# Three moves in a two-layer hybrid kernel: decay rates behind the substitution, chunk outputs in the transposes' banks, attention's value products in groups of four

## The chip, the cores and the metric

The kernel runs on one core of one Trainium2 chip. The metric is device time in microseconds (us). The kernel before took 876.38, 877.22 and 877.27 us in three runs, so its median is 877.22 us. One further execution was profiled; all durations below come from that one.

## The reference

Two layers run over 512 tokens of width 1024. Each layer normalises its input, projects it by one wide matrix, sends the pieces through three mixers of 512 channels (8 heads of 64), gates and normalises what they give, projects it back and adds it to the stream:

```python
for l in range(DEPTH):                       # 2 layers
    proj = rms_norm(h, ln_g[l]) @ w_in[l]
    u_a, z_a, u_b, z_b, q_lat, kv_lat, k_rope, z_c = jnp.split(proj, pts, axis=-1)
    y_a = rwkv7_mix(u_a, ...)                # S = S*w - (S kk) b + v k, one step a token
    y_b = rms_norm(rglru_mix(u_b, ...))      # h_t = a_t h_(t-1) + bx_t, a channel each
    y_c = rms_norm(mla_mix(q_lat, kv_lat, k_rope, ...))   # causal softmax attention
    h = h + concat([y_a*silu(z_a), y_b*silu(z_b), y_c*silu(z_c)]) @ w_out[l]
return rms_norm(h, final_g)
```

In `rglru_mix` the decay is `a = exp(-8 * gate_r * softplus(-lam))`. The vector `softplus(-lam)` depends on parameters alone, so one computation serves both layers.

## The kernel before, in words

**Arithmetic.** Each wide product is made of three matmuls (`mm3`, L231 to L233) over a high and a low half of each operand. The halves of a weight tile come from a copy on ScalarE (L140) and a subtraction on GpSimd or VectorE (L227). Some 5700 matmuls pass through TensorE (PE in the profile).

**Banks.** Matmul results go to eight banks. A rotating pool `ps` has two and serves mostly the transposes, `ck()` hands out two fixed banks in turn, and `acc` has four for the wide sums. Work on a bank waits until all that read its last contents are done.

**Order.** A compile-time scheduler lays out one instruction list for each engine from the order in which the program is written, strings of step letters and the dependences; at run time each engine takes its list strictly in order. An instruction that waits therefore holds up all behind it on its engine.

**Decay rates.** `decay_rates()` (L257 to L278) computes `softplus(-lam)` for 8 columns once, in layer 0: an exponential on ScalarE, and 25 small operations on VectorE (DVE), among them a series of seven multiply and add pairs (L272, L273). It stands behind the first list of steps of the layer. The last mask products of that list (`products`: matmuls L610, masks L613 on VectorE, transposes L628) come next on VectorE.

**Chunk stage.** The delta-rule mixer is worked in 8 chunks of 64 tokens. `substitute()` inverts 32 small triangular blocks on VectorE (L738, L740, then the transposes L743 and L745 and the copies L749). It is followed by corner products (L758, L770) and by `chunk()`: `uo` (L848) multiplies the state S, L851 adds it to the values, `so` (L858) with L862 and L863 makes the next state. After each second chunk come the outputs `yo` (L876 and L882, two banks), which VectorE copies (L884) and ScalarE squares (L885). Between these, projections and the second mixer are laid: its gate products (L688), `lru_b` (exponentials, square roots, L703 to L721, the scan L713, the squares L719 summed on GpSimd by L720), the token sums over those squares (L378), and the products for the attention's latents, which take the four `acc` banks at once.

**Attention.** For four head pairs, softmax rows are made from the scores (L1057), transposed per key block (L1076), copied by ScalarE into one of four slots (L140), and multiplied with the values (L1082) into one bank, each head into 64 of its 128 rows. Parts of the output projection are filled in between.

Of the kernel before, what the change touches and what calls it, by code (L numbers as in the profile page):

```python
# [47 lines left out]
def body(ctx, tc, x, wc, wl, wo, w2a2, gagx, wuq, wukv, vec, ln_g, fin_g, cst, out, depth=DEPTH):  # L48
# [49 lines left out]
    def ck(shape=(128, 512)):  # L98
        ckn[0] += 1
        n = 1  # L100
        for s in shape[1:]:
            n *= s
        o = cks[:, ckn[0] % 2, 0:n]
        if len(shape) == 3:
            return o.rearrange("p (a b) -> p a b", a=shape[1])
        if len(shape) == 4:
            return o.rearrange("p (a b c) -> p a b c", a=shape[1], b=shape[2])
        return o
# [11 lines left out]
    cur = [None]  # L120
    SETS = {"S": "sigmoid_and_others", "E": "natural_log_exp_and_others", "Q": "sqrt_and_others"}
    NOSYNC = mybir.DependencyInfo(mybir.DependencyClass.NoSync, mybir.DependencyReason.DATA)

    def chained(ins):
        ins = getattr(ins, "ins", ins)
# [134 lines left out]
    def decay_rates():  # L260

        lam = vecs[:, :, VO["lam"]:VO["lam"] + 4]
        l0, l1, l2, l3 = [sm([128, DEPTH, 4]) for _ in range(4)]
        V.scalar_tensor_tensor(out=l0, in0=lam, scalar=-1.0, in1=lam, op0=ALU.mult, op1=ALU.min)
        act(l1, l0, AF.Exp)
        V.tensor_scalar(out=l2, in0=l1, scalar1=2.0, scalar2=None, op0=ALU.add)
        V.reciprocal(out=l3, in_=l2)
        V.tensor_tensor(out=l1, in0=l1, in1=l3, op=ALU.mult)
        V.tensor_tensor(out=l2, in0=l1, in1=l1, op=ALU.mult)
        V.tensor_scalar(out=l3, in0=l2, scalar1=1.0 / 17.0, scalar2=1.0 / 15.0, op0=ALU.mult, op1=ALU.add)  # L270
        for n in (13, 11, 9, 7, 5, 3, 1):
            V.tensor_tensor(out=l3, in0=l3, in1=l2, op=ALU.mult)  # L272
            V.tensor_scalar(out=l3, in0=l3, scalar1=1.0 / n, scalar2=None, op0=ALU.add)  # L273
        V.tensor_tensor(out=l3, in0=l3, in1=l1, op=ALU.mult)
        V.tensor_scalar(out=l0, in0=lam, scalar1=-1.0, scalar2=0.0, op0=ALU.mult, op1=ALU.max)
        V.scalar_tensor_tensor(out=l0, in0=l3, scalar=2.0, in1=l0, op0=ALU.mult, op1=ALU.add)
        V.tensor_scalar(out=sp8, in0=l0, scalar1=8.0, scalar2=None, op0=ALU.mult)
        V.tensor_scalar(out=nsp8, in0=l0, scalar1=-8.0, scalar2=None, op0=ALU.mult)  # L278
# [41 lines left out]
    def one_layer(l):  # L320
# [328 lines left out]
        run(ORD1)  # L649


        if l == 0:
            decay_rates()
        wmod[0] = WA
        gza = []

# [68 lines left out]
        def substitute():  # L725

            X, X0 = cks.rearrange("p a (t s) -> p (a t) s", s=32), c4([128, 32, 32])
            V.transpose(out=X0.rearrange("p t s -> p (t s)"), in_=inv["D"].rearrange("p t s -> p (t s)"))
            V.tensor_copy(out=X, in_=X0)
            TT = inv["T"] = c8([128, 32, 64])  # L730
            for q in (1, 3):
                G.memset(TT[32 * q:32 * q + 32, :, 0:32], 0.0)
            tm = tl("xt", [128, 240])
            for k in range(1, 31):
                n = 31 - k
                tv = tm[:, 0:n * k].rearrange("p (t s) -> p t s", t=n)

                V.tensor_tensor(out=tv, in0=X0[:, k + 1:32, k:k + 1].to_broadcast([128, n, k]),  # L738
                                in1=X[:, k:k + 1, 0:k].to_broadcast([128, n, k]), op=ALU.mult)
                V.tensor_tensor(out=X[:, k + 1:32, 0:k], in0=X[:, k + 1:32, 0:k], in1=tv, op=ALU.add)  # L740
            V.memset(X.rearrange("p t s -> p (t s)")[:, 0:1024:33], 1.0)
            X1 = inv["X1"] = c4([128, 32, 32])
            V.transpose(out=X1.rearrange("p s y -> p (s y)"), in_=X.rearrange("p t s -> p s t"))  # L743
            TD = inv["TD"] = c4([128, 32, 32])
            V.transpose(out=TD.rearrange("p s t -> p t s"), in_=X.rearrange("p t s -> p (t s)"))  # L745
            for q in range(4):
                rows = slice(32 * q, 32 * q + 32)
                blk = q % 2
                V.tensor_copy(out=TT[rows, :, blk * 32:(blk + 1) * 32], in_=TD[rows])  # L749

        def corner_left(hf):
            go = ck([128, 16, 32])
# [87 lines left out]
        def chunk(ch):  # L840
            cp, par = ch // 2, ch % 2
            ur = slice(64 * (1 - par), 64 * (1 - par) + 64)
            if ch:
                uo = [ck([128, 4, 64]) for _ in range(2)]
                for p in range(4):
                    for e in range(2):
                        hr = slice(64 * e, 64 * e + 64)
                        PE.matmul(uo[e][ur, p, :], AR[p][hr, 0, ch * 64:(ch + 1) * 64], S[ch][hr, p, :], start=True, stop=True)  # L848
                for e in range(2):
                    u = UV[ur, :, ch, 64 * e:64 * e + 64]  # L850
                    V.tensor_tensor(out=u, in0=uo[e][ur, :, :], in1=u, op=ALU.add)  # L851
            if ch < 7:
                so = ck([128, 4, 64])
                for p in range(4):
                    for e in range(2):
                        hr = slice(64 * e, 64 * e + 64)
                        hc = slice(e * 64, (e + 1) * 64)
                        PE.matmul(so[hr, p, :], BT[p][:, ch, hc], UV[:, p, ch, hc], start=True, stop=True)  # L858
                sn = S[ch + 1] = tl("S", [128, 4, 64], bufs=3)
                pc = PC[:, :, ch:ch + 1].to_broadcast([128, 4, 64])  # L860
                if ch:
                    V.tensor_tensor(out=sn, in0=so, in1=S[ch], op=ALU.add)  # L862
                    V.tensor_tensor(out=sn, in0=sn, in1=pc, op=ALU.mult)  # L863
                else:
                    V.tensor_tensor(out=sn, in0=so, in1=pc, op=ALU.mult)
            if par == 0:
                return
            yt = c2([128, 4, 2, 64])
            sq = c2([128, 4, 2, 64])
            yo = [ck([128, 4, 64]) for _ in range(2)]  # L870

            for p in range(4):
                for e, q in ((0, 0), (1, 1), (0, 1), (1, 0)):
                    hr, uq, c = slice(64 * e, 64 * e + 64), slice(64 * q, 64 * q + 64), 2 * cp + q
                    if c:
                        PE.matmul(yo[e][uq, p, :], AR[p][hr, 1, c * 64:(c + 1) * 64], S[c][hr, p, :], start=p == 0, stop=False)  # L876
            for e in range(2):
                hc = slice(e * 64, (e + 1) * 64)
                for p in range(4):
                    for q in range(2):  # L880
                        uq, c = slice(64 * q, 64 * q + 64), 2 * cp + q
                        PE.matmul(yo[e][uq, p, :], AM[q][:, p * 8 + e * 4 + cp, 64:128], UV[:, p, c, hc], start=c == 0 and p == 0, stop=p == 3)  # L882
            for e in range(2):
                V.tensor_copy(out=yt[:, :, e, :], in_=yo[e])  # L884
                A.activation(out=sq[:, :, e, :], in_=yo[e], func=AF.Square)  # L885
            V.tensor_reduce(out=vr[:, cp, :, :], in_=sq, axis=AX.X, op=ALU.add)
            yts.append(yt)
# [180 lines left out]
        def heads(p, fill):  # L1068
            ot = ck()
            for kt in range(4):  # L1070
                n = (4 - kt) * 128
                pts = []
                for e in range(2):
                    o = ps()
                    for qt in range(kt, 4):
                        PE.transpose(o[:, (qt - kt) * 128:(qt - kt + 1) * 128], Pm[p][e, qt][:, kt * 128:(kt + 1) * 128], ident)  # L1076
                    pt = PT[:, 2 * (kt % 2) + e, :]
                    copy(pt[:, 0:n], o[:, 0:n])
                    pts.append(pt)
                fill[kt]()  # L1080
                for e in range(2):
                    PE.matmul(ot[e * 64:(e + 1) * 64, kt * 128:T], Vt[:, kt, 2 * p + e, :], pts[e][:, 0:n], start=(kt == 0), stop=(kt == 3))  # L1082
            if p == 0:
                A.activation(out=stc, in_=ot, func=AF.Square)
            else:
                sq = g2()
                A.activation(out=sq, in_=ot, func=AF.Square)
                G.tensor_tensor(out=stc, in0=stc, in1=sq, op=ALU.add)
            y = g2()
            V.scalar_tensor_tensor(out=y, in0=ot, scalar=vc("mla_g", p), in1=gzc[p], op0=ALU.mult, op1=ALU.mult)  # L1090
            yc.append(y)
# [129 lines left out]
```

## Time and profile before

| what | number |
|---|---|
| median of the runs | 877.22 us |
| the profiled execution | 874.97 us |
| its span | 873.2 us |
| TensorE busy | 804.3 us, 92% of the span |
| VectorE busy | 578.5 us, 66% |
| ScalarE busy | 502.5 us, 58% |
| GpSimd busy | 333.3 us, 38% |

The profile gives for each engine when an instruction started, how long it took, how long the engine stood idle ahead of it, and what ended that idle time. Times count from the start of the span. What decides here is the idle time of TensorE, and the few stretches in which its granted clock falls, since it is busy nearly everywhere else. Layer 0 and layer 1 run the same instruction lists but for small differences, so that a stretch of the one can be laid beside its twin in the other.

### The profile page before, as it was taken

To read this page: it belongs to the slowest core of one execution; us is meant where nothing else is said; L and a number is where in the kernel's file an instruction comes from. 1 tells how busy PE (TensorE), PEld (TensorE's weight loads), DVE (VectorE), ACT (ScalarE), POOL (GpSimd) and SP (SyncE) were. 2 spreads that over 40 slices of the span, in tenths; PEclk is the share of its full clock that TensorE was granted. 3 is DMA by queue.
4 is the path that set the end of the run, shared out by engine and by line. 5 is a ranking of instruction groups with operands and counts; after the bars stand their busy time and mean duration, and the time that the engine had idled before them with its cause. 6 is when DMAs were issued, how large, how long until landed. Compare 5 with 4: busy or idle time off the path is not lost.

```text
span 873.2 us, 15237 instructions
## 1 busy us (share of the span) xinstructions
PE 804.3 (92%) x5696; PEld 619.0 (71%) x5696; DVE 578.5 (66%) x1176; ACT 502.5 (58%) x988; POOL 333.3 (38%) x303
## 2 busy tenths in 40 slices
PE   3999997999888988999979999999999898899995
PEld 3878886886668867555768788888765696665574
DVE  5678787824887385874474776786268767677636
ACT  5667874456653535564465677845665445365634
POOL 2355554532443342010534655664133533310223
PEclk9999998999999999999999999999999999999998
DMA  6322232410112365222653222332101224731344
GB/s 221 112 73 72 70 103 86 137 62 26 42 33 91 117 209 182 72 70 94 213 190 97 73 88 91 97 112 92 38 26 41 76 95 148 235 103 49 110 166 158
DMA packets 49755, 91.08 MB, mean 104 GB/s; under 512 B 5520, under 2 KB 8336, under 8 KB 49680
## 3 DMA queue, kind: packets, MB, share of 16 engines
q1 hardware_dynamic: 49104, 89.05, 31.7%
q8 instruction: 45, 0.74, 0.4%
q10 hardware_dynamic: 576, 1.05, 0.3%
q14 instruction: 30, 0.25, 0.1%
HBM read 73.30 MB, written 16.78 MB: 103 GB/s over the span
## 4 chain that ended last, share of the span: by engine, by line
PE 64%; DVE 18%; ACT 8%; DMA 5%; issue 3%; POOL 2%; SPq 0%; ACTq 0%; DVEq 0%; POOLq 0%
PE acc L231 14%; PE acc L232 14%; PE acc L233 13%; PE acc L1057 4%; PE ck L1082 3%; PE ps L1076 3%; ACT g L137 3%; PE ps L688 2%; DMA dr<-hp 2%; DVE g L721 1%; DVE g L682 1%; DVE g L713 1%; ACT UV L140 1%; ACT wH L140 1%; PE ps L628 1%
## 5 line engine op out<-in xcount | busy, mean ns | idle before, releaser
L227 POOL TENSOR_TENSOR wL<-wr,wH 128x512 fp32r<-128x512 f32 (+1 forms) x130 | 176.1, 1359 | 308.2 <-ACT wH L140 284.4
L140 ACT ACTIVATE wH<-wr 128x512 fp32r<-128x512 f32 (+1 forms) x192 | 118.8, 621 | 144.9 <-PE acc L232 72.5
L231 PE MATMUL acc<-xH,wH 128*128 128x512 f32 (+1 forms) x496 | 193.4, 391 | 0.0
L232 PE MATMUL acc<-xL,wH 128*128 128x512 f32 (+1 forms) x496 | 189.7, 383 | 0.1
L233 PE MATMUL acc<-xH,wL 128*128 128x512 f32 (+1 forms) x496 | 189.5, 382 | 0.0
L231 PEld LDWEIGHTS acc<-xH,wH 128*128 128x128 f32 x496 | 94.8, 191 | 19.7 <-issue 1.6
L233 PEld LDWEIGHTS acc<-xH,wL 128*128 128x128 f32 x496 | 94.6, 191 | 18.9 <-issue 1.6
L232 PEld LDWEIGHTS acc<-xL,wH 128*128 128x128 f32 x496 | 94.8, 191 | 16.6 <-DVE xL L305 0.6
L227 DVE TENSOR_TENSOR wL<-wr,wH 128x512 fp32r<-128x512 f32 (+1 forms) x62 | 48.3, 779 | 64.7 <-ACT wH L140 64.5
L231 PE MATMUL acc<-wH,c 128*128 128x512 f32 x192 | 81.6, 425 | 5.3 <-DVE hp L427 5.3
L232 PE MATMUL acc<-wL,c 128*128 128x512 f32 x192 | 76.4, 398 | 0.5 <-DVE wL L227 0.5
L233 PE MATMUL acc<-wH,c 128*128 128x512 f32 x192 | 75.8, 397 | 0.0
L140 ACT ACTIVATE UV<-ps 64x512 f32<-64x512 f32 (+4 forms) x112 | 52.1, 494 | 40.4 <-PE ps L1076 31.2
L231 PEld LDWEIGHTS acc<-wH,c 128*128 128x128 f32 x192 | 36.1, 188 | 17.0 <-DVE hp L427 4.1
L140 ACT ACTIVATE c<-g 128x512 fp32r<-128x512 f32 (+1 forms) x40 | 24.8, 630 | 33.2 <-DVE g L980 27.6
L137 ACT ACTIVATE c<-acc,sm 128x128 f32<-128x128 f32 (+3 forms) x64 | 33.6, 527 | 17.8 <-DVE sm L1059 17.6
L232 PEld LDWEIGHTS acc<-wL,c 128*128 128x128 f32 x192 | 36.2, 189 | 8.6 <-issue 1.4
L1057 PE MATMUL acc<-am,am 128*128 128x128 f32 (+3 forms) x128 | 41.3, 444 | 1.1 <-ACT c L137 1.1
L233 PEld LDWEIGHTS acc<-wH,c 128*128 128x128 f32 x192 | 36.0, 188 | 8.5 <-issue 1.0
L137 ACT ACTIVATE g<-g 128x512 f32<-128x512 f32 (+1 forms) x58 | 36.2, 627 | 6.1 <-DVE g L706 4.2
L135 ACT ACT_TABLE_LOAD x29 | 37.2, 1283 | 1.2 <-PEq L1209 0.7
L368 POOL TENSOR_TENSOR g<-g,g 128x512 f32<-128x512 f32 x24 | 33.2, 1382 | 11.9 <-ACT g L137 11.9
(222 smaller groups left out, 1596.9 us busy)
## 6 DMA issues: line engine op xcount, KB each, us to landing
wr<-in_wc_dram SPq DMA_DIRECT2D x116, 256.0 KB, 2.6
wr<-in_wo_dram SPq DMA_DIRECT2D x48, 256.0 KB, 3.4
hp<-dr SPq DMA_DIRECT2D x40, 256.0 KB, 3.5
dr<-hp SPq DMA_DIRECT2D x32, 256.0 KB, 3.1
dr<-g SPq DMA_DIRECT2D x16, 256.0 KB, 2.3
g<-dr SPq DMA_DIRECT2D x16, 256.0 KB, 3.7
wr<-in_wl_dram SPq DMA_DIRECT2D x16, 208.0 KB, 2.5
c<-in_x_dram SPq DMA_DIRECT2D x8, 256.0 KB, 6.3
```

The lines of the kernel that those rows point to most:

```text
L135: chained(A.preload_act_table_set(SETS[st]))
L137: chained(A.activation(out=out, in_=in_, func=func, **kw))
L140: i = A.activation(out=out, in_=in_, func=AF.Copy, **kw)
L227: (V if wn[0] % wmod[0] == 0 else G).tensor_tensor(out=L, in0=raw, in1=f(H), op=ALU.subtract)
L231: PE.matmul(o, a[0], b[0], start=start, stop=False)
L232: PE.matmul(o, a[0], b[1], start=False, stop=False)
L233: PE.matmul(o, a[1], b[0], start=False, stop=stop)
L368: G.tensor_tensor(out=z, in0=z, in1=s, op=ALU.mult)
L688: PE.matmul(o[hr, :], gw[hr, w, j, :], xc[hr, :], start=True, stop=True)
L1057: PE.matmul(o[:, 0:n], qT[:, hd, qt * 128:n], K2[:, p, e, 0:n], start=True, stop=True)
L1076: PE.transpose(o[:, (qt - kt) * 128:(qt - kt + 1) * 128], Pm[p][e, qt][:, kt * 128:(kt + 1) * 128], ident)
L1082: PE.matmul(ot[e * 64:(e + 1) * 64, kt * 128:T], Vt[:, kt, 2 * p + e, :], pts[e][:, 0:n], start=(kt == 0), stop=(kt == 3))
```

## The change

There are three edits.

1. `decay_rates()` is called at the end of `substitute()` of layer 0 in place of behind the first list of steps, and its series is written with fused operations, 18 on VectorE where there were 25.
2. The outputs `yo` of a chunk pair take two banks of the rotating pool `ps` in place of `ck()`.
3. The value products of the attention are issued for two key blocks and both heads together, after the fill of the odd key block. The first of the four gets a dependence on the last of the four copies into the slots.

```diff
@@ decay_rates
-        V.tensor_scalar(out=l3, in0=l2, scalar1=1.0 / 17.0, scalar2=1.0 / 15.0, op0=ALU.mult, op1=ALU.add)
-        for n in (13, 11, 9, 7, 5, 3, 1):
-            V.tensor_tensor(out=l3, in0=l3, in1=l2, op=ALU.mult)
-            V.tensor_scalar(out=l3, in0=l3, scalar1=1.0 / n, scalar2=None, op0=ALU.add)
-        V.tensor_tensor(out=l3, in0=l3, in1=l1, op=ALU.mult)
+        V.tensor_scalar(out=l3, in0=l2, scalar1=1.0 / 17.0, scalar2=None, op0=ALU.mult)
+        for n in (15, 13, 11, 9, 7, 5, 3):
+            V.scalar_tensor_tensor(out=l3, in0=l3, scalar=1.0 / n, in1=l2, op0=ALU.add, op1=ALU.mult)
+        V.scalar_tensor_tensor(out=l3, in0=l3, scalar=1.0, in1=l1, op0=ALU.add, op1=ALU.mult)
@@ after run(ORD1)
-        if l == 0:
-            decay_rates()
@@ substitute, at its end
+            if l == 0:
+                decay_rates()
@@ chunk
-            yo = [ck([128, 4, 64]) for _ in range(2)]
+            yo = [ps([128, 4, 64]) for _ in range(2)]
@@ heads
-                pts = []
                 for e in range(2):
                     o = ps()
                     for qt in range(kt, 4):
                         PE.transpose(...)
-                    pt = PT[:, 2 * (kt % 2) + e, :]
-                    copy(pt[:, 0:n], o[:, 0:n])
-                    pts.append(pt)
+                    last_pt = copy(PT[:, 2 * (kt % 2) + e, 0:n], o[:, 0:n])
                 fill[kt]()
-                for e in range(2):
-                    PE.matmul(ot[e * 64:(e + 1) * 64, kt * 128:T], Vt[:, kt, 2 * p + e, :], pts[e][:, 0:n], start=(kt == 0), stop=(kt == 3))
+                if kt % 2 == 0:
+                    continue
+                for k2 in (kt - 1, kt):
+                    for e in range(2):
+                        i = PE.matmul(ot[e * 64:(e + 1) * 64, k2 * 128:T], Vt[:, k2, 2 * p + e, :], PT[:, 2 * (k2 % 2) + e, 0:(4 - k2) * 128],
+                                      start=(k2 == 0), stop=(k2 == 3))
+                        if k2 < kt and e == 0:
+                            tc.add_manual_dep(i.ins, last_pt.name, SYNC, reason="one group")
```

The scheduler lays the lists out anew. In the changed kernel's file most lines are one number higher at first (L231 is L232, L613 stays) and two lower from `gate_a` on (L688 is L686, L705 is L703).

**VectorE, layer 0, ahead of the last mask products.** Before (`am` is the masked product, `sm` the 8 columns of the decay rates):

```order
L594 TENSOR_TENSOR g_169_789<-ps_1200,g_187_873 128x512
L272 TENSOR_TENSOR sm_1210<-sm_1210,sm_1209 128x8
L210 TENSOR_TENSOR c_319_1505<-g_220_1027,c_318_1504 128x512
L273 TENSOR_SCALAR sm_1210<-sm_1210 128x8
...
L274 TENSOR_TENSOR sm_1210<-sm_1210,sm_1208 128x8
L276 SCALAR_TENSOR_TENSOR sm_1207<-sm_1210,sm_1207 128x8
L277 TENSOR_SCALAR sp_102<-sm_1207 128x8
L278 TENSOR_SCALAR nsp_103<-sm_1207 128x8
L613 TENSOR_TENSOR am_317<-ps_1336,C 128x512
```

With the change, the same place:

```order
L592 SCALAR_TENSOR_TENSOR g_220_1027<-g_220_1027,vecs,g_229_1069 128x512
L594 TENSOR_TENSOR g_169_789<-ps_1200,g_187_873 128x512
L211 TENSOR_TENSOR c_315_1475<-g_220_1027,c_314_1474 128x512
L613 TENSOR_TENSOR am_317<-ps_1306,C 128x512
L613 TENSOR_TENSOR am_317<-ck,C 128x512
```

The small operations have left the place ahead of the first mask product; they now stand between the last steps of the substitution and behind its transposes.

**TensorE, layer 0, at the token sums.** `acc_2798` to `acc_2801` before, and `acc_2801` to `acc_2804` with the change, are the four banks of the latents. Before, the sums (L378) stand between products of all four, behind the last chunk:

```order
L231 MATMUL acc_2801<-wH_2842,xH_104 128x416
L232 MATMUL acc_2801<-wL_2843,xH_104 128x416
L233 MATMUL acc_2801<-wH_2842,xL_105 128x416
L231 MATMUL acc_2798<-wH_2860,xH_104 128x416
L232 MATMUL acc_2798<-wL_2861,xH_104 128x416
L378 MATMUL ck<-ones_96,sqn_2232 128x2 x4
```

With the change (`ps_3130` are the first transposes of the chunk outputs):

```order
L234 MATMUL acc_2803<-wH_2863,xL_105 128x416
L978 MATMUL ps_3130<-C,c_406_2267 128x128
L978 MATMUL ps_3130<-C,c_412_2342 128x128
L978 MATMUL ps_3130<-C,c_432_2484 128x128
L978 MATMUL ps_3130<-C,c_437_2556 128x128
L378 MATMUL ck<-ones_96,sqn_2227 128x2 x4
L232 MATMUL acc_2804<-wH_2809,xH_104 128x416
L233 MATMUL acc_2804<-wL_2810,xH_104 128x416
```

All products of the fourth bank, and half of those of the other three, now stand behind the token sums. The gate products of `lru_b(2, 3)`, on whose results the sums depend, moved from between the second and third chunk pairs to behind the last chunk; between them and the sums stand 12 matmuls of 512 columns and 36 of 416, beside the transposes shown. On VectorE and ScalarE the work of `lru_b(2, 3)` moved behind the last chunk in the same way.

**TensorE, layer 0, first head pair of the attention.** Before, each key block's two products (L1082) stand together:

```order
L1057 MATMUL acc_3754<-am_3119,am_3121 128x512
L231 MATMUL acc_3763<-wH_3606,c_550_3134 128x512
L232 MATMUL acc_3763<-wL_3607,c_550_3134 128x512
L233 MATMUL acc_3763<-wH_3606,c_550_3134 128x512
L1082 MATMUL ck<-UV_3120 64x384 x2
L1076 MATMUL ps_3770<-C,c_654_3557 128x128
```

With the change the products are L1083:

```order
L1057 MATMUL acc_3755<-am_3122,am_3124 128x512
L1083 MATMUL ck<-UV_3123 64x512
L232 MATMUL acc_3764<-wH_3609,c_558_3137 128x512
L233 MATMUL acc_3764<-wL_3610,c_558_3137 128x512
L234 MATMUL acc_3764<-wH_3609,c_558_3137 128x512
L1083 MATMUL ck<-UV_3123 64x512
L1083 MATMUL ck<-UV_3123 64x384 x2
L1075 MATMUL ps_3777<-C,c_664_3562 128x128
```

The first product of a group stands alone and the other three follow together after other matmuls, in the first three head pairs; the 256 and 128 column products of the later key blocks stand together in all four.

More of the change, by code (lines that the diff above doesn't have):

```diff
@@ L122, in body @@
     NOSYNC = mybir.DependencyInfo(mybir.DependencyClass.NoSync, mybir.DependencyReason.DATA)
+    SYNC = mybir.DependencyInfo(mybir.DependencyClass.Sync, mybir.DependencyReason.DATA)
     def chained(ins):
```

## The prediction

> **What bounds the kernel now.** I read the page first, then the waits of TensorE (PE), then stretches of the timeline, with layer 1 beside layer 0.
>
> ```profile
> span 873.2 us, 15237 instructions
> PE 804.3 (92%) x5696; PEld 619.0 (71%) x5696; DVE 578.5 (66%) x1176; ACT 502.5 (58%) x988; POOL 333.3 (38%) x303
> PE ck L848 <- ACT c L885: 12.8, 4, 4.3
> PE ps L628 <- DVE am L613: 6.1, 3, 5.0
> ```
>
> TensorE is busy 92% of the span, so an edit pays by the idle time of TensorE that it removes, or by matmul time. A row of waits gives total, times and longest. Two of them bear on the change: 12.8 us ahead of L848, where a chunk wants a bank from which ScalarE has not yet squared the outputs, and 6.1 us ahead of L628, behind masks that VectorE (DVE) is late with. Stages that no edit names keep their work, with the order a little shifted; I take nothing for them.
>
> **Decay rates.** Columns are start, duration, engine, line, operation, count, and in brackets the idle time before.
>
> ```profile
> 131.10 1.25 DVE L273 TENSOR_SCALAR sm<-sm 128x8 f32<-128x8 f32 x1
> 136.20 0.17 DVE L272 TENSOR_TENSOR sm<-sm,sm 128x8 f32<-128x8 f32 x1
> 138.38 0.68 DVE L613 TENSOR_TENSOR am<-ps,C 128x512 f32<-128x512 f32 x1
> 139.12 1.11 PE L628 MATMUL ps<-C,c 128*128 128x128 f32 x4 [4.98 <-DVE am L613]
> 132.09 0.37 PE L610 MATMUL ps<-c,c 64*128 64x128 f32 x1
> 563.05 0.37 PE L610 MATMUL ps<-c,c 64*128 64x128 f32 x1
> 169.15 2.02 PE L785 MATMUL ps<-UV,am 64*64 64x64 f32 x62
> 592.31 0.86 PE L785 MATMUL ps<-UV,am 64*64 64x64 f32 x22
> 130.00:140.00 10.00, 5.02 (x38) 4.04 (x36) 9.49 (x21) 4.33 (x8) 6.07 (x5) 0.92 0.46 158
> 140.00:150.00 10.00, 10.00 (x41) 8.30 (x40) 5.34 (x13) 4.56 (x8) 3.18 (x3) 0.74 0.00 1
> ```
>
> The series of small operations runs from 131.1 to 138.4 in front of the first mask L613; TensorE stands still 4.98 us and then runs at a granted clock of 0.74 (the windows give PE, PEld, DVE, ACT and POOL busy, then that clock). Layer 1 has no series: from the same L610 to the same L785 it takes 592.31 - 563.05 = 29.26 us, layer 0 169.15 - 132.09 = 37.06. The list of TensorE is the same there before and after, so layer 0 should do as its twin: **-7.8 us**.
>
> The new place has to hide it. Layer 1 shows that place without the series:
>
> ```profile
> 590.67 0.63 ACT L137 ACTIVATE g<-g 128x512 f32<-128x512 f32 x1
> 593.51 0.60 ACT L140 ACTIVATE c<-ps 128x512 f32<-128x512 f32 x1 [0.63 <-PE ps L785]
> 594.74 1.25 DVE L743 STREAM_TRANSPOSE c<-ck 128x1024 f32<-128x1024 f32 x1
> 598.00 4.88 DVE L749 COPY c<-c 32x1024 f32<-32x1024 f32 x4
> 599.91 1.03 PE L795 MATMUL ps<-C,c 128*128 128x128 f32 x8
> 609.45 1.98 PE L758 MATMUL ck<-c,am 32*32 32x32 f32 x64
> L135 ACT ACT_TABLE_LOAD x29 | 37.2, 1283 | 1.2 <-PEq L1209 0.7
> ```
>
> Behind the sigmoid that ends at 591.30 ScalarE now has a table load (1.28), the exponential (0.2) and a second load (1.28), and is free at about 594.1. The copy due at 593.51 is 0.6 us late; L795 needs it at 599.91. VectorE comes to the reciprocal's inputs about 1 us too early, then does some 15 operations of 0.17 (1.25 where GpSimd works beside it, as at 131.10) between the substitution's own: 3 to 7 us. The transposes L743 then end near 600 to 603 in place of 596, for L758 at 609.45; the copies L749 near 606 to 610 in place of 602.9, for products that come behind those of L758. Both are covered. If no cover were there it would cost 4 to 5 us. Range of this part: -8.5 to -3.
>
> **Chunk outputs.** Layer 0, the longest stall and what made it:
>
> ```profile
> 255.57 2.28 DVE L713 TENSOR_TENSOR_SCAN g<-g,g 128x512 f32<-128x512 f32 x1 [0.96 <-POOL g L711]
> 259.21 0.35 PE L232 MATMUL acc<-wL,xH 128*128 128x416 f32 x1
> 259.40 0.35 PE L233 MATMUL acc<-wH,xL 128*128 128x416 f32 x1
> 259.22 3.37 DVE L721 SCALAR_TENSOR_TENSOR g<-g,vecs,g 128x512 f32<-128x512 f32 x2
> 262.52 0.41 DVE L884 COPY c<-ck 128x256 f32<-128x256 f32 x1
> 264.27 0.88 PE L848 MATMUL ck<-S,c 64*64 64x64 f32 x16 [4.34 <-ACT c L885]
> 265.94 0.55 PE L231 MATMUL acc<-wH,xH 128*128 128x416 f32 x1
> 260.00:270.00 10.00, 5.73 (x47) 5.12 (x48) 7.06 (x10) 4.86 (x10) 7.04 (x6) 0.83 0.20 48
> 243.63 1.93 PE L688 MATMUL ps<-g,w 64*64 64x512 f32 x8 [0.50 <-DVE g L682]
> 258.59 3.45 POOL L720 TENSOR_TENSOR sqn<-sqn,g 128x512 f32<-128x512 f32 x2 [1.82 <-ACT g L719]
> ```
>
> The copies of `yo` (L884) stand on VectorE behind the `lru_b` work that waits on GpSimd, the squares behind the copies, and L848 behind the squares. With other banks for `yo` this wait goes: 12.8 us over two layers, 6.4 each. After the long stall the clock is 0.83 and matmuls of 416 columns follow each other at 0.35 us in place of 0.19 (259.21 to 259.40), about nine of them: 1.4 us more. Removed: **7.8 us a layer**.
>
> What comes in its place is read from the order. (a) Chunks now follow each other as fast as the state allows: L851 (0.42), L858, L862 (0.42), L863 (0.4 to 1.1) and the hand-overs, against three to six matmuls of filling. Small idle times of this kind are 1.65 us now (the 0.50 above is the largest of six); laying the new order out by the rows' durations I get 3.7: +2.0, from +0.5 to +3. (b) Smaller pieces between chunks mean more changes of matmul shape, about 0.1 each (0.33 in place of 0.23, below): +0.5, at most 0.8. (c) The token sums. They now wait for gate products that come last in the stage. Before, from the end of those products (243.63 + 1.93 = 245.56) to the last sum of squares on GpSimd (258.59 + 3.45 = 262.04) it took 16.5 us; with less chunk work mixed in but the group norm in front I lay it out at 15 to 16. TensorE's cover between is 12 matmuls at 0.23, 36 at 0.19 and 0.6 for four transposes, 10.1 us. New idle time 5.4 us, from 2.4 (a chain of 12.5) to 7.4 (17.5). (d) The clock after it: 1.4 us as after the 4.34 stall, up to 2.6 as in the window after the 4.98 one (0.26 of 10 us); none if the wait is short. I take 1.6.
>
> So -7.8 + 2.0 + 0.5 + 5.4 + 1.6 = **+1.7 us a layer, +3.4 in all**; ends -4.4 and +6 a layer.
>
> [...]
>
> **Value products.** Starts in the third and fourth head pairs of layer 0; layer 1 reads alike.
>
> ```profile
> 391.32 1.07 PE L1082 MATMUL ck<-UV 128*64 128x512 f32 x2
> 392.33 0.70 PE L1057 MATMUL acc<-am,am 128*128 128x256 f32 x2
> 406.44 0.40 PE L233 MATMUL acc<-wH,c 128*128 128x512 f32 x1
> 406.77 1.24 PE L1082 MATMUL ck<-UV 128*64 128x512 f32 x4
> 407.94 0.87 PE L1076 MATMUL ps<-C,c 128*128 128x128 f32 x6
> 418.00 0.44 PE L1082 MATMUL ck<-UV 128*64 128x128 f32 x4
> 418.37 0.50 PE L231 MATMUL acc<-wH,c 128*128 128x512 f32 x1
> 418.71 0.40 PE L232 MATMUL acc<-wL,c 128*128 128x512 f32 x1
> 418.94 0.39 PE L233 MATMUL acc<-wH,c 128*128 128x512 f32 x1
> ```
>
> One head's 512 columns alone take 1.01 us to the next start, both heads together 1.17: the two halves of the array run side by side. A wide matmul takes 0.23 but 0.33 ahead of such a group and 0.34 behind it, and 128 columns of a pair still take 0.37. A group therefore has about 0.36 us of fixed cost (0.10, 0.10 and a start-up of 0.16), saved where two become one: five times a layer (four times 256 with 128, and 512 with 384 in the last pair), 1.8 us. In the first three pairs the first product now stands alone. That gains about 1.0 us in the second and third pairs, where the heads are apart already, and loses 0.7 in the first, where they were together. The next transposes now stand close behind the last (two banks, ScalarE's copies at 0.5): 0.6 us lost. Sum -1.5 a layer, **-3 in all**, ends -5 and +1.
>
> **The sum.** The profiled execution took 874.97 us, 1.8 more than its span and 2.25 less than the median. 874.97 - 7.8 + 3.4 - 3.0 = 867.6; against the median 877.2 - 7.4 = **869.8 us**.
>
> **Rivals.** First, *the chunk edit pays in full*: the token sums' chain is short enough for its cover. For it: VectorE has no chunk work mixed into the chain any more. Against it: 16.5 against 10.1. Then (c) and (d) go, -5.3 a layer: 877.2 - 7.8 - 10.6 - 3 = 856. Second, *the token sums cost more than the bank did*: the group norm's four scalings, slowed by GpSimd's multiplications as L721 was (3.37 for two), hold the chain back. Slower than before by 0.2% is 879.0, 9.2 us over the forecast or 4.6 a layer, a chain of over 20 us; at 21.5 the stall is 11.4, the chunk edit +7.7 a layer: 877.2 - 7.8 + 15.4 - 3 = 882. Against it: the scalings end at about the time at which the second table load does. Third, *the series is late in its new place too*: the loads and GpSimd hold up the copy for L795 or the transposes for L758, and 4 to 5 us come back: 874 to 875. Against it: the cover of 5 to 13 us in layer 1.
>
> **How the numbers follow.** The forecast's own range is 864 to 876, with 0.58; the first rival has 0.18 (852 to 864), the second 0.11 (over 879), the third 0.13 (873 to 878). 0.2% is 1.75 us, about what can be told from no change. Faster takes the forecast, the first rival and a part of the third: 0.77; within 0.2%, 0.12; slower 0.11. The range is 857 to 878.
>
> **What would show it.** TensorE's wait ahead of L628 is gone and L610 to L785 of layer 0 takes 29.3 us; L758 has no idle time. No wait of L848 on L885; a new one at L378 of 2 to 7 us in each layer, with a clock under 1 behind it. The value products fall into eleven groups a layer. It would be wrong if L378 does not wait (856), or by over 10 us (882), or if layer 0 keeps its lag on layer 1.

## The result

The changed kernel took 869.26 us (median of four runs, 868.69 to 870.45), against 876.8 us for four runs of the kernel before: a ratio of 0.9918 with a 95% interval from 0.9901 to 0.9935, so it is 0.7 to 1.0% faster. 869.8 was forecast. The profiled execution took 868.69 us, its span is 866.8 us, 6.4 less than the 873.2 of before. The profiled execution of before (874.97 us) lies 1.8 us under that kernel's median, the one of the changed kernel 0.6 under, so the profiles differ by less than the medians.

The page of the changed kernel:

```profile
span 866.8 us, 15212 instructions
PE 801.0 (92%) x5696; PEld 624.3 (72%) x5696; DVE 574.6 (66%) x1169; ACT 506.2 (58%) x990; POOL 332.3 (38%) x303
```

Those of its waits of TensorE that bear on the change (total, times, longest). Line numbers are those of the changed file:

```profile
PE ck L378 <- POOL sqn L718: 10.4, 2, 5.2
PE ck L848 <- DVE S L863: 4.1, 4, 1.2
PE acc L233 <- DVE wL L228: 4.0, 3, 1.5
PE ps L882 <- DVE UV L851: 3.5, 5, 1.0
PE ps L628 <- DVE am L613: 1.1, 2, 0.6
```

The 12.8 us of L848 behind the squares are gone, and so is the 5.0 us stall of L628. In their place stand 5.2 us a layer ahead of the token sums, and three smaller groups of waits that belong to the chunk stage, but for 1.1 us of the third row (L233), which lie between the layers.

To see what each stage does, the table takes the starts of five landmarks from TensorE's timelines: the first L785, the first L848, the first score product of the attention (L1057), its token sums, and the first L785 of layer 1. Two numbers are layer 0 and layer 1. The last three columns are the runs with one edit each, told below.

| stage, us | before | changed | decay alone | chunk alone | values alone |
|---|---|---|---|---|---|
| start to L785 | 169.15 | 161.50 | 161.48 | 169.12 | 170.95 |
| L785 to L848 | 50.17, 50.20 | 50.17, 50.19 | 50.20, 50.19 | 50.16, 50.22 | 50.16, 50.22 |
| L848 to L1057 | 131.53, 131.19 | 134.94, 134.35 | 131.18, 131.78 | 135.15, 132.63 | 131.88, 130.37 |
| L1057 to the attention's sums | 73.10, 72.68 | 71.06, 71.06 | 72.63, 72.60 | 72.65, 72.61 | 71.60, 71.04 |
| the sums to L785 of layer 1 | 168.36 | 167.22 | 168.19 | 167.70 | 167.32 |
| last sums to the end | 26.82 | 26.31 | 26.45 | 27.06 | 25.96 |

The difference of the spans is -7.65 ahead of L785, +3.41 and +3.16 in the stages of the chunks, -2.04 and -1.62 in the attention, -1.14 between the layers and -0.51 at the end: -6.4. The stage between the layers is not edited in any column and still differs by 1.1 us among them. The start of the run with the value products alone is not edited either and is 1.8 us longer than before: behind the same stall at L628 (5.00 and 4.98 us) its granted clock from 140 to 150 us is 0.60 in place of 0.74. So a single profile tells a stage to no better than about 2 us.

**Decay rates.** The changed kernel, TensorE and VectorE at the old place, then at the new:

```profile
132.24 0.37 PE L610 MATMUL ps<-c,c 64*128 64x128 f32 x1
133.44 0.69 DVE L613 TENSOR_TENSOR am<-ps,C 128x512 f32<-128x512 f32 x1 [3.65 <-PE ck L610]
134.22 0.66 PE L628 MATMUL ps<-C,c 128*128 128x128 f32 x4
161.50 2.08 PE L785 MATMUL ps<-UV,am 64*64 64x64 f32 x64
162.05 0.17 DVE L267 TENSOR_SCALAR sm<-sm 128x8 f32<-128x8 f32 x1 [1.19 <-ACT sm L138]
166.23 1.25 DVE L741 STREAM_TRANSPOSE c<-ck 128x1024 f32<-128x1024 f32 x1
178.64 1.98 PE L758 MATMUL ck<-c,am 32*32 32x32 f32 x64
```

VectorE now waits for TensorE at L613 in place of the other way round, and L610 to L785 takes 161.50 - 132.24 = 29.26 us. At the new place VectorE waits 1.19 us for the exponential. The transposes L741 start at 166.23, 2.3 us later than in the twin when the landmarks are laid over each other (594.74 - 592.31 + 161.50 = 163.93), and TensorE asks for them at 178.64 without idle time.

**Chunk stage.** The chain of the second mixer in the changed kernel, from its gate products (L686) to its sums of squares on GpSimd (L718); L894 are the group norm's scalings:

```profile
250.39 1.93 PE L686 MATMUL ps<-g,w 64*64 64x512 f32 x8
255.64 4.19 DVE L894 TENSOR_TENSOR c<-c,vr 128x512 f32<-128x512 f32 x4
262.26 0.46 PE L233 MATMUL acc<-wL,xH 128*128 128x416 f32 x1 [1.44 <-DVE wL L228]
266.53 3.10 POOL L718 TENSOR_TENSOR sqn<-sqn,g 128x512 f32<-128x512 f32 x2 [1.82 <-ACT g L717]
269.68 1.87 PE L378 MATMUL ck<-ones,sqn 128*128 128x2 f32 x8 [5.21 <-POOL sqn L718]
272.60 0.55 PE L232 MATMUL acc<-wH,xH 128*128 128x416 f32 x1
272.94 0.55 PE L233 MATMUL acc<-wL,xH 128*128 128x416 f32 x1
```

From 250.39 + 1.93 = 252.32 to 266.53 + 3.10 = 269.63 the chain takes 17.3 us. TensorE stands still for 5.21 us, and goes on at 0.35 us for each matmul of 416 columns. The stretch from the first L848 to the first product behind the latents, as windows (length, then busy time of PE, PEld, DVE, ACT and POOL, the granted clock, DMA share and GB/s), of the kernel before:

```profile
219.32:288.33 69.01, 60.94 (x647) 48.30 (x647) 53.22 (x101) 35.45 (x59) 29.25 (x24) 0.98 0.20 60
642.51:711.00 68.49, 60.42 (x645) 47.71 (x645) 52.71 (x100) 34.99 (x58) 28.74 (x24) 0.98 0.19 57
```

and of the changed kernel:

```profile
211.67:284.56 72.89, 62.18 (x652) 50.45 (x652) 55.41 (x101) 35.63 (x59) 29.86 (x24) 0.95 0.18 53
635.08:707.50 72.42, 62.00 (x650) 50.24 (x650) 55.03 (x100) 35.39 (x59) 30.18 (x24) 0.95 0.16 49
```

Both layers lose 3.9 us there. In layer 0 the idle time goes from 69.01 - 60.94 = 8.07 to 72.89 - 62.18 = 10.71 us, and the same work is busy 1.24 us longer at a clock of 0.95.

**Value products.** A loose group of the first head pair and the whole group of the last, in the changed kernel (a row counts two instructions for each product):

```profile
361.93 1.07 PE L1083 MATMUL ck<-UV 128*64 128x512 f32 x2
362.93 0.50 PE L232 MATMUL acc<-wH,c 128*128 128x512 f32 x1
363.84 1.72 PE L1083 MATMUL ck<-UV 128*64 128x512 f32 x6
365.49 0.44 PE L1075 MATMUL ps<-C,c 128*128 128x128 f32 x2
403.97 1.73 PE L1083 MATMUL ck<-UV 128*64 128x512 f32 x8
405.62 0.66 PE L1075 MATMUL ps<-C,c 128*128 128x128 f32 x4
```

Three products together (512, 384 and 384 columns) take 1.65 us to the next start, and four also take 1.65. So the single product that runs ahead costs 1.0 us more, and would be nearly free if it stood with the others.

### The profile page after: what moved, and what is told of

It is laid out like the page before. It is cut to its first block, busy times and chain, and to the rows that moved or that the text cites. A ratio compares the mean times of both kernels' runs of the same rounds, so it can differ in the third digit from the quotient of the medians.

```text
span 866.8 us, 15212 instructions
## 1 busy us (share of the span) xinstructions
PE 801.0 (92%) x5696; PEld 624.3 (72%) x5696; DVE 574.6 (66%) x1169; ACT 506.2 (58%) x990; POOL 332.3 (38%) x303
## 4 chain that ended last, share of the span: by engine, by line
PE 43%; DVE 10%; ACT 5%; DMA 3%; issue 2%; POOL 2%; SPq 0%; ACTq 0%; DVEq 0%; POOLq 0%
PE acc L232 9%; PE acc L233 9%; PE acc L234 9%; PE acc L1057 4%; PE ck L1083 3%; PE ps L1075 2%; DMA hp<-dr 1%; ACT g L138 1%; DMA wr<-in_wo_dram 1%; ACT UV L141 1%; DVE c L460 1%; PE ps L686 1%; PE ps L610 1%; ACT wH L141 1%; DVE wL L228 1%
## 5 line engine op out<-in xcount | busy, mean ns | idle before, releaser
L232 PE MATMUL acc<-xH,wH 128*128 128x512 f32 (+1 forms) x496 | 191.4, 387 | 0.0
L233 PE MATMUL acc<-xL,wH 128*128 128x512 f32 (+1 forms) x496 | 189.8, 383 | 0.4 <-DVE xL L305 0.3
L232 PEld LDWEIGHTS acc<-xH,wH 128*128 128x128 f32 x496 | 94.0, 190 | 19.2 <-issue 1.6
L233 PEld LDWEIGHTS acc<-xL,wH 128*128 128x128 f32 x496 | 94.3, 190 | 17.6 <-DVE xL L305 1.2
L232 PE MATMUL acc<-wH,c 128*128 128x512 f32 x192 | 83.7, 436 | 2.5 <-DVE hp L427 1.2
L233 PE MATMUL acc<-wL,c 128*128 128x512 f32 x192 | 77.6, 404 | 1.1 <-DVE wL L228 1.1
L234 PE MATMUL acc<-wH,c 128*128 128x512 f32 x192 | 77.3, 403 | 0.0
L232 PEld LDWEIGHTS acc<-wH,c 128*128 128x128 f32 x192 | 37.2, 194 | 12.8 <-ACT c L141 2.9
L233 PEld LDWEIGHTS acc<-wL,c 128*128 128x128 f32 x192 | 37.1, 193 | 9.5 <-DVE wL L228 1.5
L1057 PE MATMUL acc<-am,am 128*128 128x128 f32 (+3 forms) x128 | 42.3, 447 | 0.9 <-ACT c L138 0.8
L234 PEld LDWEIGHTS acc<-wH,c 128*128 128x128 f32 x192 | 36.9, 192 | 8.6 <-issue 0.5
L368 POOL TENSOR_TENSOR g<-g,g 128x512 f32<-128x512 f32 x24 | 32.6, 1360 | 10.4 <-ACT g L138 10.4
```

Source lines behind the costliest of these rows:

```text
L232: PE.matmul(o, a[0], b[0], start=start, stop=False)
L233: PE.matmul(o, a[0], b[1], start=False, stop=False)
L234: PE.matmul(o, a[1], b[0], start=False, stop=stop)
L368: G.tensor_tensor(out=z, in0=z, in1=s, op=ALU.mult)
L1057: PE.matmul(o[:, 0:n], qT[:, hd, qt * 128:n], K2[:, p, e, 0:n], start=True, stop=True)
```

## The experiments

**One edit at a time.** Each run takes one of the three parts of the diff shown above and leaves the rest of the kernel as before.

```diff
+ decay_rates(): shorter series, called at the end of substitute()      # decay alone
```

> The decay rates alone: moved behind the substitution with the shorter series, all else as before. Theory (the moved series is hidden, the parts add up): 7.8 us less than before, from TensorE's first L610 of that stage to its first L785 29.3 us where it took 37.06. Rival (the series is late in its new place too, or part of the gain needs the other edits): 3 to 5 us less.

Measured: 867.7 us, ratio 0.9908 (0.9892 to 0.9924), 7 to 9 us less, as the theory has it; L785 starts at 161.48 in place of 169.15. The series is hidden at its new place, and the twin layer gave the size.

```diff
-            yo = [ck([128, 4, 64]) for _ in range(2)]
+            yo = [ps([128, 4, 64]) for _ in range(2)]                   # chunk alone
```

> The chunk outputs' banks alone. Theory (the wait of the chunks on the squares goes, and a longer one at the token sums comes): slower than before, by 3.4 us as predicted or up to 6.6 us as the stages of the changed kernel read, with a wait of about 5 us ahead of the token sums in each layer. Rival (the stall at the token sums only shows because the other edits came too): 5 to 12 us faster.

Measured: 882.02 us, ratio 1.0071 (1.0045 to 1.0096): alone, this edit makes the kernel slower, by 6 us in the medians. Its waits of TensorE:

```profile
PE ck L378 <- POOL sqn L720: 10.4, 2, 5.2
PE ck L848 <- DVE S L863: 4.1, 4, 1.2
```

These are the rows of the changed kernel again, so the stall at the token sums comes from this edit and not from the other two.

```diff
+ heads(): value products after each odd key block, four together       # values alone
```

> The value products in groups alone. Theory: 3 to 3.7 us less than before, 1.6 to 2.0 us a layer between the first scores (L1057) and the token sums of the attention. Rival (the groups only save what new waits on copies take back): within 1 us of before.

Measured: 873.38 us, ratio 0.9966 (0.9949 to 0.9982), 1.6 to 4.5 us less, with 1.50 and 1.64 us of it in the attention's stages. The rival is out; the gain is at or a little under the theory's lower end.

```diff
-            yo = [ps([128, 4, 64]) for _ in range(2)]
+            yo = [ck([128, 4, 64]) for _ in range(2)]                   # changed kernel, this part undone
```

> The changed kernel with the chunk outputs put back into the two fixed banks. Theory (that edit costs, the other two pay): 3.4 to 6.6 us less than the changed kernel, 863 to 866 us, no wait at the token sums, and the chunk's wait of 12.8 us back. Rival (the edit pays): 872 or more.

Measured: 865.24 us, ratio to before 0.988 (0.9845 to 0.9914), 4.0 us under the changed kernel. The intervals of the two overlap; the direction agrees with the run of the edit alone. Its wait of the chunks is back:

```profile
PE ck L848 <- ACT c L885: 12.9, 4, 4.3
```

**What holds TensorE at the token sums.** First, the sums held behind all products of the latents:

```diff
-    ORD3 = "... N0 A2 B1 g0 g1 R0 t0 t6 t1 t2 t4 Y0 t5 t3 t7 T0 g2 g3 T1"
+    ORD3 = "... N0 A2 B1 g0 g1 t0 t6 t1 t2 t4 Y0 t5 t3 t7 T0 R0 g2 g3 T1"
+    tc.add_manual_dep(<first matmul of L378>, <last product of the latents>, NOSYNC)
```

> The changed kernel with the token sums (L378) held behind all products of the latents. Theory A (the sums' place on TensorE's list is the stall): the 5.2 us ahead of them and the slow clock behind go in both layers, 13 us less than the changed kernel, 856 us. Theory B (the fourth bank of the latents waits for the same chain, since ScalarE drains it behind the squares): the wait moves to the first product of that bank and 1 to 3 us are won in all, 866 to 868 us.

Measured: 870.02 us, ratio 0.9927 (0.9901 to 0.9953), no faster than the changed kernel. ScalarE and TensorE of this run:

```profile
267.48 0.58 ACT L141 ACTIVATE g<-acc 128x512 f32<-128x512 f32 x1
268.12 0.71 PE L234 MATMUL acc<-wH,xH 128*128 128x416 f32 x1 [4.16 <-ACT g L141]
268.63 0.55 PE L235 MATMUL acc<-wL,xH 128*128 128x416 f32 x1
```

The wait moved from the sums to the first product of the latents' fourth bank, as theory B has it. ScalarE drains that bank behind the squares of the same chain, and the 4.16 us are followed by slow matmuls too (0.35 us between starts, and 0.19 from 274.34 us on). So the sums are only the first of two places at which the late chain is felt. The 1 to 3 us that theory B expected did not come; 3.0 us of waits for weights from GpSimd, which the changed kernel does not have, stand against them.

Second, the chain itself earlier, and the sums late as in the run before:

```diff
-    ORD3 = "... A3 H4 H5 H6 H7 N0 A2 B1 g0 g1 R0 t0 ... t7 T0 g2 g3 T1"
+    ORD3 = "... A3 H4 A2 H5 B1 H6 H7 N0 g0 g1 t0 ... t7 T0 R0 g2 g3 T1"
```

> As the run with the late token sums, and the last gate products written ahead of the sixth chunk, the rest of that mixer's work ahead of the seventh, in place of behind the last. Theory (what the chunk banks lose is the late state chain): no wait at the sums and none at the fourth bank, 848-to-1057 some 126 to 129 us a layer in place of 134.9, so 857 to 862 us in all. Rival (VectorE's work of that mixer delays the chunk states as it did before the change): a wait of the chunks on VectorE of over 5 us a layer, 866 us or more.

Measured: 861.02 us, ratio 0.9826 (0.9797 to 0.9855), 8.2 us under the changed kernel. From L848 to L1057 it takes 130.03 and 130.35 us, 4 to 5 less than the changed kernel, and TensorE waits neither at the sums nor at the fourth bank. The rival was half right: VectorE holds back the last chunk's values for 3.5 us, once a layer, but the time is not the rival's. This written order was not tried with the old banks, where the scheduler lays these gate products early by itself.

```profile
257.75 1.97 PE L886 MATMUL ps<-UV,am 128*64 128x64 f32 x30 [3.46 <-DVE UV L855]
255.00:260.00 5.00, 2.25 (x31) 2.13 (x32) 5.00 (x6) 2.41 (x4) 3.10 (x3) 0.73 0.20 80
260.00:265.00 5.00, 5.00 (x25) 4.71 (x25) 4.97 (x9) 3.18 (x7) 3.87 (x4) 0.93 0.00 0
```

Third, the group norm's scalings, which stand ahead of the chain's VectorE work, held behind the scans:

```diff
-    ORD3 = "... H7 N0 A2 B1 g0 g1 R0 ..."
+    ORD3 = "... H7 A2 B1 N0 g0 g1 R0 ..."
+    tc.add_manual_dep(<each scaling of group_norm>, <last scan of lru_b>, NOSYNC)
```

> The changed kernel with the group norm's four scalings (4.2 us on VectorE) held behind the scans of the second mixer. Theory (the scalings hold the state chain back by about 2 us): from the end of the gate products to the last sum of squares about 15 us in place of 17.3, 2 to 4 us less in all if the cover stays. Rival (GpSimd and the table loads set the chain): 17 us as before. The order of TensorE shifts too, with nine matmuls fewer ahead of the sums, 1.7 us less cover, so the chain is what is read.

Measured: 872.17 us, ratio 0.9951 (0.9933 to 0.9969), 2.9 us over the changed kernel, where 2 to 4 us less were expected if the cover stayed. TensorE's gate products, GpSimd's sums and TensorE's next wait:

```profile
252.66 1.93 PE L686 MATMUL ps<-g,w 64*64 64x512 f32 x8
266.76 3.11 POOL L720 TENSOR_TENSOR sqn<-sqn,g 128x512 f32<-128x512 f32 x2 [1.82 <-ACT g L719]
268.89 0.45 PE L982 MATMUL ps<-C,c 128*128 128x128 f32 x1 [6.00 <-DVE c L896]
```

The chain is 266.76 + 3.11 - 254.59 = 15.3 us in place of 17.3, so the scalings did hold it back by 2.0. But TensorE now waits for the scaled outputs themselves, which the scheduler still places ahead of the sums. These waits are 14.3 us in all, against 10.4 at the sums of the changed kernel, so the gain in the chain is spent there and more.

**The groups of value products.** The first product of each group is held behind the last matmul of the fill, so that nothing comes between:

```diff
                         if k2 < kt and e == 0:
                             tc.add_manual_dep(i.ins, last_pt.name, SYNC, reason="one group")
+                            tc.add_manual_dep(i.ins, <last matmul of the fill>, NOSYNC, reason="one group")
```

> The changed kernel with the first value product of each group held behind the matmuls of the fill, so that four stand together in all groups but one. Theory (a group of three takes as long as one of four, 1.65 us, so the single first product's 1.0 us and its two changes of shape are lost): 1.0 to 1.2 us less for each of two groups a layer, 4 to 5 us less than the changed kernel, 865 us. Rival (the matmuls that the first product let through earlier now wait for banks): no gain, 869 us.

Measured: 864.42 us, ratio 0.9869 (0.9831 to 0.9907), 4.8 us under the changed kernel, the intervals just overlapping. The attention's stages take 68.81 and 68.85 us in place of 71.06 twice. Its group of the first head pair, in the timeline of TensorE:

```profile
363.53 1.72 PE L1085 MATMUL ck<-UV 128*64 128x512 f32 x8
365.18 0.50 PE L234 MATMUL acc<-wH,c 128*128 128x512 f32 x1
```

All four products, eight instructions, are one group and take 1.65 us, as the theory has it.

**The repairs together.** First the held groups with the decay rates moved and the chunk outputs as before, then all three edits with both repairs.

```diff
+ decay_rates() moved, value groups held; yo = [ck(...)] as before
```

> Decay rates moved, value products in held groups, chunk outputs in the two fixed banks as before. Theory: 4 to 5 us less than with the loose groups, 860 to 861 us, the fastest so far. Rival: 865 us, as with the loose groups.

Measured: 860.67 us, ratio 0.9823 (0.9795 to 0.9852), as the theory has it.

```diff
+ all three edits, groups held, ORD3 = "... A3 H4 A2 H5 B1 H6 H7 N0 g0 g1 t0 ... T0 R0 ..."
```

> All three edits, with the last gate products ahead of the sixth chunk, the token sums late, and the value groups held. Theory (the two repairs lie in different stages and add up): 861.0 less 4 to 5 us, 856 to 857 us, the fastest of all. Rival: 860 us or more.

Measured: 860.44 us, ratio 0.9812 (0.9774 to 0.9851), with runs from 856.64 to 862.99. The median is the rival's, and the interval reaches down to the theory's 857, so whether the two repairs add up stays open. The attention got shorter as expected (69.43 and 68.99 us), but L848 to L1057 longer by 2.2 and 1.6 us than in the run without held groups, though TensorE's list there is the same. The granted clock of these stages is 0.96 in both layers, against 0.99 and 0.97; the last section comes back to it.

```diff
+ all three edits, groups held, ORD3 = "... A3 H4 H5 A2 B1 H6 H7 N0 g0 g1 t0 ... T0 R0 ..."
```

> As the run with both repairs, with the last gate products ahead of the seventh chunk. In the run with the sixth, VectorE's work of that mixer holds the last chunk's values back for 3.5 us (L886 behind L855). Theory (a chunk later, this wait becomes shorter and nothing else waits): 1 to 3 us a layer less, 851 to 855 us. Rival (the fourth bank of the latents then waits for the chain): the same or slower, 857 to 860 us.

Measured: 859.12 us, ratio 0.9804 (0.9786 to 0.9822), runs from 858.54 to 859.67: the lowest median here, 1.2% under the changed kernel and 2% under the kernel before. The median is the rival's again: the wait for the last chunk's values falls to 1.6 us, but weights from VectorE then come late for 5.4 us in all, and a bank of the latents waits for ScalarE, 0.26 us in layer 0 and 1.76 in layer 1. Its interval overlaps those of the two runs before.

**What of the decay rates pays.**

```diff
+ decay_rates(): shorter series, called where it was
```

> The kernel before with the shorter series of the decay rates, at its old place. Theory (the place matters, the number of operations little): of the 7.8 us some 1.4 to 3 us are won, 7 operations at 0.2 to 0.4 us, 874 us. Rival (the shorter series is what pays): 7 us or more.

Measured: 875.3 us, ratio 0.9984 (0.9968 to 1.0001). VectorE and TensorE at that place:

```profile
131.58 5.25 DVE L272 SCALAR_TENSOR_TENSOR sm<-sm,sm 128x8 f32<-128x8 f32 x6
138.16 1.12 PE L627 MATMUL ps<-C,c 128*128 128x128 f32 x4 [3.54 <-DVE am L612]
```

Six of the fused operations still take 5.25 us. In the kernel before, four of the small operations took 1.13 to 1.25 us each while GpSimd worked (129.3 to 136.1 us), and those behind it 0.17. The stall falls from 4.98 to 3.54 us. The gain is 1.4 us in the medians and not clear of zero, so nearly all of the 7.7 us comes from the place. The long series at the new place was not tried.

## Why the prediction was right, and where it was not

**Decay rates: right, by the twin layer.** -7.8 was forecast, -7.65 came in the profile. The wait for the exponential (about 1 us forecast, 1.19 measured) and the cover were as worked out. The transposes came 2.3 us late where 3 to 7 were forecast: at the new place all but one of the operations ahead of them take 0.2 us or less. The third rival fell with it: neither L758 nor L795 waits for VectorE or ScalarE.

**Chunk outputs: the right mechanism, the wrong size.** +3.4 us over two layers was forecast, +6.6 came in this pair of profiles. The wait of 12.8 us went as said. Of what came in its place, term by term, in layer 0:

- (a), the chunks' own waits: +2.0 forecast. In layer 0 of the changed kernel they are 4.05 us in place of 1.65, so +2.4.
- (c), the stall at the token sums: 5.4 forecast, 5.21 measured. It is a near hit for two reasons that cancel, which is luck. The chain is 17.3 us and not 15 to 16, since the scalings hold it back by 2.0; and the cover is 12.1 and not 10.1, mostly by a wait that the sum did not have.
- That wait is the term that was left out: the latents' products wait 1.44 us for weights whose low half stands on VectorE behind the scalings and the first work of `lru_b`.
- (d), the clock: 1.6 us forecast. Some ten products at 0.35 in place of 0.19 are 1.6, and the token sums themselves take 1.73 us to the next start in place of 0.81: 2.5 in all.

So -7.8 + 2.4 + 5.2 + 1.4 + 2.5 = +3.7 a layer, against 3.9 measured in this stretch; about 0.2 is left for (b), forecast at 0.5. The windows bear the sum out: the waits come to -6.4 + 2.4 + 5.2 + 1.4 = +2.6 us, as the idle time has it (8.07 to 10.71), and the clock to 2.5 - 1.4 = +1.1, near the 1.24 us of longer busy time. The rest of the way to L1057 gives some 0.5 us back.

The 6.6 us hang on the clock of these two executions too. The whole stage from L848 to L1057 in layer 0, before and changed, in windows as above:

```profile
219.32:350.85 131.53, 117.17 (x896) 92.92 (x896) 91.99 (x185) 65.57 (x120) 50.02 (x38) 0.97 0.36 114
211.67:346.61 134.94, 120.22 (x896) 96.83 (x895) 94.23 (x185) 66.09 (x120) 48.59 (x38) 0.94 0.35 112
```

Idle time is nearly the same over it (14.36 and 14.72 us), since TensorE waits 2.3 us less behind the latents than before. Of the 3.4 us, 3.05 are longer busy time, at a lower clock. In layer 1 of the run with this edit alone the same stage takes 132.63 us, at a clock of 0.97, with the same waits. Six profiles on record have the old banks and no edit in this stage (before, decay alone, values alone, decay and values, that with held groups, the short series in place): 130.37 to 132.95 us, 131.6 on average. Three have the new banks and no other edit there (changed, chunk alone, held groups): 132.39 to 135.15, 134.0 on average. So the edit costs about 2.4 us a layer, 4.8 in all. That lies between the 4.0 and the 6.0 us of the medians, and is more than the forecast still.

**Value products: right in all, by errors that cancel.** -3 was forecast, -3.7 came. In layer 1, where the stage lost 1.62 us, the starts tell the terms apart. The five merged groups won 0.9 us to their next starts, and the wide matmuls around them 0.3, where 1.8 was forecast: 256 with 128 columns win 0.16 and not 0.36. The product that now stands alone gained 1.1 us in the second and third pairs, as forecast, and lost 0.4 in the first, where 0.7 was. The transposes lost about 0.35 and not 0.6. So the mis-sized term is the fixed cost of a group, and smaller losses made up for it. The sum implies about 1.7 us for the three products, and they take 1.65; that a fourth beside them would be free was not seen. Holding the groups together is what this part had left to give.

**The total is partly luck.** -7.4 was forecast and about -7.5 came, but in the profiles the chunk edit cost 3.2 us more than its term, the attention gave 0.7 more, and 1.6 us come from stages that no edit names, for which I had taken nothing. That leaves -6.4; the other 1.1 us is that the profile of before lies further under its median than that of the changed kernel does.

**The first rival**, that the chunk edit pays in full, did not happen, but the run with the early gate products shows under which condition it comes near: 861.0 with the edit and the order with early gates, 865.2 without either. With held groups the same comparison is 859.1 against 860.7. The intervals overlap both times, so what the edit is worth at its best stays open between nothing and about 4 us; the written order with early gates has no run without the edit. **The second rival** named the scalings as the cause; they cost 2.0 us of chain, too little for a slower kernel in all. That the chunk edit alone is slower, 882 us, is what the forecast's sign for this term said, and it was hidden in the total by the decay rates.

## What to carry to other kernels

Where two layers run the same list, the stage without the edited work is a good measure of what that work costs; here it was right to 0.2 us. A wait that a free bank removes need not vanish when a compile-time scheduler lays out the order anew: look in the new list for the work that the old wait had let pass in time, follow that chain to whoever needs its end, and count the banks and weights that wait for it too, not only the first consumer. When small products take much less time in a group than one by one, hold the whole group together: here four took 1.65 us, and so did three, and the one that ran ahead cost its full 1.0 us.

## What the runs showed that I had not expected

In these runs stalls of one length did not bring one clock. The runs with early gates, loose and held, have the same list in this stretch and nearly the same stall, 3.46 (shown above) and 3.45 us. The run with held groups:

```profile
257.17 1.97 PE L886 MATMUL ps<-UV,am 128*64 128x64 f32 x30 [3.45 <-DVE UV L855]
255.00:260.00 5.00, 2.83 (x32) 2.61 (x33) 5.00 (x6) 2.41 (x4) 3.50 (x3) 0.58 0.09 34
260.00:265.00 5.00, 5.00 (x21) 4.64 (x20) 4.90 (x11) 3.28 (x7) 2.75 (x3) 0.74 0.00 0
```

Its clock is 0.58 and then 0.74, against 0.73 and 0.93. And in the changed kernel the clock fell to 0.50 at the second of two short pauses, at the latents' transposes:

```profile
308.43 0.63 PE L961 MATMUL ps<-C,g 128*128 128x128 f32 x4 [0.62 <-DVE g L979]
310.30 0.77 PE L232 MATMUL acc<-wH,c 128*128 128x512 f32 x1 [1.23 <-ACT c L141]
310.86 0.63 PE L233 MATMUL acc<-wL,c 128*128 128x512 f32 x1
311.29 0.63 PE L234 MATMUL acc<-wH,c 128*128 128x512 f32 x1
```

while before the change pauses of 0.53 and 1.30 us at the same place left it at 1.00:

```profile
311.93 0.66 PE L961 MATMUL ps<-C,g 128*128 128x128 f32 x4 [0.53 <-DVE g L979]
313.88 0.47 PE L231 MATMUL acc<-wH,c 128*128 128x512 f32 x1 [1.30 <-DVE hp L427]
314.19 0.39 PE L232 MATMUL acc<-wL,c 128*128 128x512 f32 x1
314.42 0.39 PE L233 MATMUL acc<-wH,c 128*128 128x512 f32 x1
```

Matmuls follow each other at 0.43 us in the first and 0.23 in the second. In the changed kernel the clock is 1.00 from 306.0 to 309.4 us and 0.50 from there to 314.0, so it falls inside the second pause. Term (d) of the prediction took a short wait to cost no clock; this one of 1.23 us did, and the one of 1.30 did not. Why it falls there was not shown.

The spread of one kernel's runs, up to some 6 us, goes at least in part with the clock: of the ten runs of the values alone the fastest, 869.79 us, has a granted clock of 0.983, and the two slowest, 875.69 and 875.73 us, have 0.975. One of 873.70 us has 0.974, so the clock is not all of it. What makes the clock differ between runs was not shown.
